# Opening of a two-layer backbone on one NeuronCore: the modulation in two halves of channels, two token pairs in between, and the transposed banks read by VectorE alone

## The chip, the core and the metric

The kernel runs on one core of one Trainium2 chip. A core has five engines that each work through their own instruction queue in order: TensorE (PE in the profile, with its weight loads as PEld), VectorE (DVE), ScalarE (ACT), GpSimd (POOL) and SyncE (SP, which here only starts transfers between the chip's memory and the on-chip memory). Semaphores hold an instruction back until what it needs is done. TensorE writes its results into eight banks of a small memory (PB in the profile) of 128 partitions by 512 fp32 words each; VectorE and ScalarE read them from there. The metric is the device time of one execution in microseconds, the median over runs.

## What is computed

Two layers over 1024 latent tokens and 256 context tokens of width 1024; layer 0 is windowed attention with sink logits, layer 1 latent attention. What the change touches is the very beginning of layer 0: a modulated normalization of all 1280 tokens, and its product with the value columns of the layer's input weight.

```python
def rms_norm(u, g):
    uf = u.astype(F32)
    y = uf * lax.rsqrt(jnp.mean(uf * uf, axis=-1, keepdims=True) + EPS)
    return (y * g.astype(F32)).astype(u.dtype)

def adaln(cond, w, bias):
    m = jax.nn.silu(cond) @ w + bias
    return jnp.split(m, 3, axis=-1)            # shift, scale, gate
...
    shift_x, scale_x, gate_x = adaln(c, ada_w[i], ada_b[i])
    shift_c, scale_c, gate_c = adaln(c_ctx, ada_w[i], ada_b[i])
    hx = rms_norm(x, norm_g[i]) * (1.0 + scale_x[:, None]) + shift_x[:, None]
    hc = rms_norm(ctx, norm_g[i]) * (1.0 + scale_c) + shift_c
    ...                                        # then h @ a_w_in[0], of which columns 1280:1536 are the values
```

All of it is fp32. A product is made from three matmuls of a high and a low part of each operand (high times high, low times high, high times low), so each tensor that TensorE multiplies is first split into its high part (a cast by ScalarE) and its low part (a subtraction).

## The kernel before

The whole kernel is laid out so that TensorE is never without work once the modulated tokens are there: the projections of layer 0, its attention, then layer 1. The stretch before that is the opening. Its order is written out by hand, for every engine, by the order of the calls in the code (a manual schedule): an engine takes its instructions in the order in which the lines issue them.

The opening handles the 1280 tokens as five pairs of 128-token tiles, `p` = 0 (context) to 4. The channels of a pair are worked in four groups `b` of 256 channels, so there are 20 groups, `g` = 0 to 19. The steps, by the names in the code:

- `ada_load(k)`, `ada_mm(k)`: 128 rows of the modulation weight (1 MB, two transfers of 512 KB) are loaded into one of three buffers, and TensorE multiplies them with both conditioning vectors; eight `k` make the sum over the 1024 input channels. `ada_cols` (L677 to L691) copies the sum, turns it to columns on TensorE and forms the factors A and B of all 1024 channels.
- `x_load(i)`, `norm(i)`: a tile of 128 tokens (512 KB) is loaded; ScalarE squares and sums it (L700), GpSimd makes the reciprocal root in two small instructions (L701, L702), and VectorE forms a diagonal matrix with it (L704), called the diagonal below.
- `turn(g)`: four matmuls of token tile times diagonal (L716) write 256 normalized channels of both tiles, transposed, into one bank. The first of them needs the pair's first diagonal, the next the second.
- `h_part(g)`: both halves of the bank are read twice, by ScalarE, which writes the high part of A·x+B directly (L728), and by VectorE, which writes A·x+B in fp32 (L729); the subtraction (L730) then gives the low part, on VectorE for even `g` and on GpSimd for odd `g`. Two engines that read the same bank are kept apart by semaphores, so the four readings of a group take turns.
- `v_part(g)`: twelve matmuls (L126 to L128, 256 wide) add the group's part of the values; after the fourth group of a pair, ScalarE and VectorE split the pair's values out of their bank into V, in four instructions. This split is called the V drain below.
- `w0_load`, `w0_cut`: the value columns of the weight (two transfers of 512 KB) and their split.

The loop at the end of the opening issues, at step `g`: `turn(g + 2)`, `h_part(g)`, then at the first two steps of each pair the `norm` of the next pair's tiles, and `v_part(g - 2)`. It runs after `ada_cols`, so that all 20 groups wait for the last row of the modulation weight. Some steps of the loop also start the transfers and the splits of the next weight block (`fetch(1)`, `next_item`). After the loop come the projections, which need the modulated tokens of pair 0 first.

Of the kernel before, what the change touches and what calls it, by code (L numbers as in the profile page):

```python
# [18 lines left out]
D = 1024  # L19
# [40 lines left out]
def kernel(ctx: ExitStack, tc: tile.TileContext, t, out, dbg=None):  # L60
# [593 lines left out]
    awr = Ring(F, [0, 8, 16], 2048)  # L654
    xs = Ring(F, [24, 28, 32, 36], 1024)
    w0 = f_at(40, 8, 256)
    am = f_at(22, 512)
    dg = Ring(F, [48, 48.5, 49, 49.5], 128)
    junk = f_at(50, 512).bitcast(BF16)
    hr = Ring(F, [16, 18, 20, 14], 512)  # L660
    PA, PM = PB[:, 6, :], PB[:, 7, :]
    turned = [0, 1, 2, 3, 6, 7]
    aw, xn, os = {}, {}, {}

    def ada_load(k):
        aw[k] = awr.next()
        for c in (0, 1024):
            load(out=aw[k][:, c : c + 1024], in_=t["ada_w"][0, k * 128 : k * 128 + 128, c : c + 1024])

    def ada_mm(k):  # L670
        for q in (0, 1, 2, 3):
            nc.tensor.matmul(
                PA[32 * q : 32 * q + 2], sc[:, k, :], aw[k][:, q * 512 : q * 512 + 512], start=k == 0, stop=k == 7
            )

    def ada_cols():
        nc.scalar.copy(am, PA)  # L677
        for j in range(4):
            nc.tensor.transpose(PM[:, j * 128 : j * 128 + 128], am[:, j * 128 : j * 128 + 128], ident)
        m = PM.rearrange("p (j q r) -> p q j r", j=4, q=4)[:, :, :, 0:2]  # L680

        def both(ap):
            return ap.rearrange("p (h j) c -> p h j c", h=2)

        def wide(ap):
            return ap.rearrange("p (h j) -> p h j", h=2).unsqueeze(3).to_broadcast([128, 2, 4, 2])

        A, B = both(ada0.A), both(ada0.B)
        nc.vector.tensor_add(A, m[:, 2:4], wide(adab[:, 0, 8:16]))
        nc.vector.scalar_tensor_tensor(A, A, 1.0, wide(ng[:, 0, :]), ALU.add, ALU.mult)  # L690
        nc.vector.tensor_add(B, m[:, 0:2], wide(adab[:, 0, 0:8]))  # L691

    def x_load(i):
        xn[i] = [xs.next(), None]
        load(out=xn[i][0], in_=src0(i))

    def norm(i):

        st = sm_ring()
        nc.scalar.activation(junk, xn[i][0], AF.Square, accum_out=st[:, 0:1])  # L700
        nc.gpsimd.tensor_scalar(st[:, 1:2], st[:, 0:1], 1.0 / D, EPS, ALU.mult, ALU.add)  # L701
        nc.gpsimd.tensor_tensor(st[:, 2:3], st[:, 1:2], mhalf, ALU.pow)  # L702
        xn[i][1] = dg.next()
        nc.vector.tensor_scalar_mul(xn[i][1], ident, st[:, 2:3])  # L704

    def bank(g):
        return shp(PB[:, turned[g % 6], :], 2, 256)

    def turn(g):

        p, b = g // 4, g % 4
# [8 lines left out]
    def h_part(g, eng):  # L720
        p, b = g // 4, g % 4
        w = 1 if p == 0 else 0
        h = shp(hr.next(), 2, 256)
        hi = hT[p][:, 0, 2 * b : 2 * b + 2, :]
        for kk in range(2):
            k = 2 * b + kk
            sa, sb = ada0.A[:, k, w : w + 1], ada0.B[:, k, w : w + 1]
            nc.scalar.activation(hi[:, kk], bank(g)[:, kk], AF.Identity, bias=sb, scale=sa)  # L728
            nc.vector.tensor_scalar(h[:, kk], bank(g)[:, kk], sa, sb, ALU.mult, ALU.add)  # L729
        eng.tensor_sub(hT[p][:, 1, 2 * b : 2 * b + 2, :], h, hi.bitcast(F32))  # L730

    def v_part(g):


        p, b = g // 4, g % 4
# [24 lines left out]
    nc.vector.memset(PA, 0.0)  # L760
    ada_load(0)
    load_small()
    ada_load(1)
    x_load(0)
    x_load(1)
    ada_load(2)
    w0_load(0)
    ada_mm(0)
    ada_mm(1)
    norm(0)  # L770
    norm(1)
    ada_mm(2)
    ada_load(3)
    w0_load(1)
    w0_cut(0)
    w0_cut(1)
    for g in range(2):
        turn(g)
    ada_load(4)
    ada_mm(3)  # L780
    ada_load(5)
    for g in range(2, 4):
        turn(g)
# [822 lines left out]
```

## Time and profile before

| | |
|---|---|
| median of three runs | 1646.34 us (1645.45 to 1647.07) |
| profiled execution, its own time | 1645.1 us |
| its span in the profile | 1643.1 us |
| TensorE busy in the span | 1583.2 us (96%) |
| factors A and B of all channels ready, first modulated bank | 34.77 us |
| last wait of TensorE in the opening ends | 98.35 us |
| granted clock of TensorE, mean of the span | 0.989 |

The page of the profile gives busy times by engine, a time line in 40 slices, the chain of work that ended last, and groups of instructions by line. A row of the time line reads: start, duration, engine, line, operation, what it writes and reads, how many instructions are merged, and in square brackets how long the engine was idle before and what ended that. A row of the table by windows has, after the window and its length, the busy microseconds and instruction counts of PE, PEld, DVE, ACT and POOL, then the granted clock of TensorE (1.00 is full speed), the share of the transfer engines' time and the transfer rate in GB/s.

### The profile page before, as it was taken

The page shows a single profiled execution, that of the slowest core. Times are in us where ns is not written, and L with a number is a line of the kernel's source. Part 1 is how long each engine was busy: PE and PEld are TensorE (multiplying, and loading weights), DVE is VectorE, ACT ScalarE, POOL GpSimd, SP SyncE. Part 2 cuts the span into 40 slices and gives each one's busy share as a digit, 9 for nine tenths or more (in the row PEclk, how much of TensorE's full clock was granted, in tenths as well). Part 3 has the DMA queues.
Part 4 walks back from the last instruction along what each step waited for, and adds up shares of the span by engine and source line. Part 5 has one row for each costly group of instructions (what it writes and reads, how often), then busy time and mean ns, then how long its engine had stood idle before and what let it go on. Part 6 is the DMA issues. An engine that isn't in the chain of part 4 may idle for free.

```text
span 1643.1 us, 23681 instructions
## 1 busy us (share of the span) xinstructions
PE 1583.2 (96%) x8232; PEld 1222.1 (74%) x8232; DVE 948.1 (58%) x1724; ACT 810.8 (49%) x1732; POOL 807.9 (49%) x865
## 2 busy tenths in 40 slices
PE   5899999989999999999999999999999999999998
PEld 1888888777888888878887887566756756666687
DVE  1567868837767777769444015655555455455354
ACT  2531212228777777777333334555555555555421
POOL 1442535415554334445245422786676777668510
PEclk8899999989999999999999999999999999999999
DMA  8325544573333322235127712210111111122151
GB/s 310 116 92 191 182 145 167 158 229 116 100 113 100 94 91 91 90 119 167 52 80 248 236 62 90 74 55 33 39 39 36 46 38 37 46 80 69 47 160 65
DMA packets 120351, 176.74 MB, mean 108 GB/s; under 512 B 11420, under 2 KB 71452, under 8 KB 120232
## 3 DMA queue, kind: packets, MB, share of 16 engines
q1 hardware_dynamic: 112952, 164.31, 30.6%
q10 hardware_dynamic: 7280, 10.92, 2.0%
q8 instruction: 65, 1.06, 0.3%
q14 instruction: 54, 0.44, 0.1%
HBM read 129.04 MB, written 46.15 MB: 107 GB/s over the span
## 4 chain that ended last, share of the span: by engine, by line
PE 81%; DVE 6%; ACT 4%; DMA 3%; issue 3%; POOL 2%; SPq 0%; ACTq 0%; POOLq 0%; DVEq 0%
PE PB L126 17%; PE PB L128 17%; PE PB L127 16%; PE PB L1279 9%; PE PB L570 5%; PE PB L1245 4%; PE PB L560 4%; PE PB L533 2%; PE PB L534 2%; DMA arena_f<-ada_w 2%; DVE arena_f L729 1%; DVE arena_f L344 1%; PE PB L1304 1%; DVE arena_r L122 1%; ACT arena_f L1264 1%
## 5 line engine op out<-in xcount | busy, mean ns | idle before, releaser
L126 PE MATMUL PB<-arena_r 128*128 128x512 f32 (+3 forms) x1632 | 608.0, 373 | 3.4 <-ACT arena_r L205 2.1
L127 PE MATMUL PB<-arena_r 128*128 128x512 f32 (+3 forms) x1632 | 595.9, 365 | 2.3 <-POOL arena_r L730 1.6
L128 PE MATMUL PB<-arena_r 128*128 128x512 f32 (+3 forms) x1632 | 594.3, 366 | 0.2 <-DVE arena_r L122 0.2
L126 PEld LDWEIGHTS PB<-arena_r 128*128 128x128 f32 (+1 forms) x1632 | 310.4, 190 | 90.7 <-issue 32.0
L1271 POOL TENSOR_TENSOR arena_f<-arena_f 128x512 f32<-128x512 f32 x252 | 327.5, 1300 | 75.1 <-ACT arena_f L1264 60.0
L128 PEld LDWEIGHTS PB<-arena_r 128*128 128x128 f32 (+1 forms) x1632 | 309.4, 190 | 48.9 <-DVE arena_r L122 0.4
L127 PEld LDWEIGHTS PB<-arena_r 128*128 128x128 f32 (+1 forms) x1632 | 310.4, 190 | 43.6 <-POOL arena_r L730 2.0
L1264 ACT ACTIVATE arena_f<-PB 128x512 f32<-128x512 f32 x320 | 189.1, 598 | 124.9 <-PE PB L128 113.2
L1249 DVE TENSOR_REDUCE arena_f<-PB 128x1 f32<-128x1280 f32 x128 | 190.4, 1488 | 103.9 <-PE PB L1245 101.4
L122 DVE TENSOR_TENSOR arena_r<-PB,arena_r 128x512 fp32r<-128x512 f32 (+4 forms) x255 | 163.0, 646 | 131.5 <-ACT arena_r L121 129.7
L122 POOL TENSOR_TENSOR arena_r<-arena_f,arena_r 128x512 fp32r<-128x512 f32 x80 | 111.2, 1403 | 176.3 <-ACT arena_r L121 160.7
L121 ACT CAST arena_r<-PB 128x512 fp32r<-128x512 f32 (+4 forms) x255 | 139.2, 550 | 78.8 <-PE PB L560 38.9
L540 DVE CUSTOM_DVE_ANT_0 arena_f<-PB,arena_f,small 128x256 f32<-128x256 f32 (+1 forms) x288 | 145.3, 523 | 32.1 <-PE PB L534 25.0
L1279 PE MATMUL PB<-arena_f 128*64 128x512 f32 x640 | 157.1, 600 | 0.0
L541 ACT ACTIVATE arena_f<-arena_f,small 128x640 f32<-128x640 f32 (+2 forms) x160 | 118.9, 744 | 28.2 <-DVE small L540 27.1
L570 PE MATMUL PB<-arena_r 128*128 128x512 f32 x336 | 120.9, 436 | 4.5 <-ACT arena_f L581 4.1
L344 DVE SCALAR_TENSOR_TENSOR arena_f<-arena_f,small 128x512 f32<-128x512 f32 x98 | 114.8, 1217 | 4.1 <-DMA arena_f<-ada_w 3.8
L560 PE MATMUL PB<-ident,arena_f 128*128 128x128 f32 x672 | 104.8, 273 | 0.4 <-ACT arena_f L541 0.3
L121 ACT CAST arena_r<-arena_f 128x512 fp32r<-128x512 f32 (+1 forms) x120 | 69.5, 607 | 71.4 <-DMA arena_f<-a_w_in 22.6
L1279 PEld LDWEIGHTS PB<-arena_f 128*64 128x64 f32 x640 | 43.5, 136 | 81.0 <-issue 79.5
L1245 PE MATMUL PB<-arena_r 96*128 96x512 f32 (+1 forms) x384 | 99.8, 367 | 0.3 <-DVE arena_f L1249 0.2
L560 PEld LDWEIGHTS PB<-ident,arena_f 128*128 128x128 f32 x672 | 82.6, 140 | 15.0 <-ACT arena_f L541 1.5
(163 smaller groups left out, 1734.1 us busy)
## 6 DMA issues: line engine op xcount, KB each, us to landing
arena_r<-q_d SPq DMA_DIRECT2D x148, 128.0 KB, 2.7
arena_f<-ada_w SPq DMA_DIRECT2D x64, 256.0 KB, 3.1
arena_f<-a_w_in SPq DMA_DIRECT2D x36, 256.0 KB, 2.9
arena_f<-ada_w SPq DMA_DIRECT2D x16, 512.0 KB, 8.7
arena_f<-x SPq DMA_DIRECT2D x16, 512.0 KB, 6.6
q_d<-arena_f SPq DMA_DIRECT2D x16, 512.0 KB, 3.0
qn_d<-arena_f SPq DMA_DIRECT2D x16, 512.0 KB, 5.1
arena_r<-qn_d SPq DMA_DIRECT2D x32, 256.0 KB, 3.5
```

The costliest lines, as they stand in the source:

```text
L121: nc.scalar.copy(hi, src)
L122: (lo_eng or nc.vector).tensor_sub(lo, src, hi.bitcast(F32))
L126: nc.tensor.matmul(o, ah, bh, start=first, stop=False)
L127: nc.tensor.matmul(o, al, bh, start=False, stop=False)
L128: nc.tensor.matmul(o, ah, bl, start=False, stop=last)
L560: nc.tensor.transpose(pt[:, h, :], self.Ps[h][:, ci * 128 : ci * 128 + 128], ident)
L570: nc.tensor.matmul(self.pv, V[:, self.chunks[ci], self.g, :], PT[:, s], start=ci == 0 and s == 0, stop=ci == self.m - 1 and s == 1,)
L1245: nc.tensor.matmul(psm[:, n0 : n0 + n], self.qT[0:96, 0, b * 128 : b * 128 + 128], kt[0:96, 0, n0 : n0 + n], start=True, stop=True,)
L1249: nc.vector.reduce_max(self.mx[:, 96 + b : 97 + b], psm[:, 0:TOK], AX.X, negate=True)
L1264: nc.scalar.activation(E, S, AF.Exp)
L1271: eng.tensor_add(self.acc, self.acc, E)
L1279: nc.tensor.matmul(self.pv[p : p + 64], Vq[:, c, self.h % 4, :], self.E.pop(c), start=c < 2, stop=c >= NT - 2)
```

## The change

**Modulation in two halves.** The modulation weight is loaded and multiplied as two halves `h` of 512 channels: `ada_load(h, k)` brings 512 KB in one transfer, with rows of 2 KB from two places in place of rows of 4 KB, into one of four buffers of that size, and `ada_mm(h, k)` has two matmuls where there were four; there are 16 of each. `ada_cols(h)` forms the factors of 512 channels, with a copy and transposes of 34 rows, by the method `set_cols` that layer 1 already uses, and runs twice.

**Two pairs in between.** The 20 groups get another order, held in `parts`: first the groups of channels 0 to 511 of pairs 0 and 1 (numbers 0 to 3), which need the first half only, then those of channels 512 to 1023 of the same pairs (4 to 7), then pairs 2 to 4 as before. Numbers 0 to 3, and `turn` of 4 to 7, are issued between the multiplications of the second half, and the loads of the second half are issued among them.

**Banks read by VectorE alone.** `h_part` has VectorE write A·x+B for both halves of the bank to on-chip memory, and ScalarE casts the 512 words from there to the high part in one instruction (L723). `h_low` does the subtraction one step later (L728), on GpSimd for three groups of four and on VectorE for the fourth. In the V drain, ScalarE makes both copies before VectorE makes both subtractions. `bank` uses four banks in place of six.

**Order of the loop.** `h_part(g)` stands ahead of `turn(g + 2)`; the diagonal is split off as `diag` and stands two steps after the pair's first `norm`, behind `h_part`. Buffers move to other places, and `x_load`, `fetch(1)` and the tables for the rotation are issued one or two steps later.

```diff
+    awr = Ring(F, [0, 4, 8, 12], 1024)
...
+    parts = [(p, b) for h in range(2) for p in range(2) for b in (2 * h, 2 * h + 1)]
+    parts += [(p, b) for p in range(2, NP) for b in range(4)]
...
+    def ada_load(h, k):
+        aw[h, k] = shp(awr.next(), 2, 512)
+        src = t["ada_w"][0, k * 128 : k * 128 + 128, 0 : 2 * D].rearrange("p (a c) -> p a c", a=2)
+        load(out=aw[h, k], in_=src[:, :, h * 512 : h * 512 + 512])
+    def ada_mm(h, k):
+        for a in range(2):
+            nc.tensor.matmul(PA[32 * a : 32 * a + 2], sc[:, k, :], aw[h, k][:, a, :], start=k == 0, stop=k == 7)
+    def ada_cols(h):
+        nc.scalar.copy(am[0:34], PA[0:34])
         for j in range(4):
+            nc.tensor.transpose(PM[:, 34 * j : 34 * j + 34], am[0:34, j * 128 : j * 128 + 128], ident[0:34, 0:34])
+        m = shp(PM, 4, 34)
+        ada0.set_cols(m[:, :, 32:34], 1, h)
+        ada0.set_cols(m[:, :, 0:2], 0, h)
...
+    def h_part(g):
+        p, b = parts[g]
         w = 1 if p == 0 else 0
+        hs[g] = shp(hr.next(), 2, 256)
         for kk in range(2):
             k = 2 * b + kk
             sa, sb = ada0.A[:, k, w : w + 1], ada0.B[:, k, w : w + 1]
-            nc.scalar.activation(hi[:, kk], bank(g)[:, kk], AF.Identity, bias=sb, scale=sa)
-            nc.vector.tensor_scalar(h[:, kk], bank(g)[:, kk], sa, sb, ALU.mult, ALU.add)
-        eng.tensor_sub(hT[p][:, 1, 2 * b : 2 * b + 2, :], h, hi.bitcast(F32))
+            nc.vector.tensor_scalar(hs[g][:, kk], bank(g)[:, kk], sa, sb, ALU.mult, ALU.add)
+        nc.scalar.copy(hT[p][:, 0, 2 * b : 2 * b + 2, :], hs[g])
+    def h_low(g, eng):
+        p, b = parts[g]
+        ks = slice(2 * b, 2 * b + 2)
+        eng.tensor_sub(hT[p][:, 1, ks, :], hs[g], hT[p][:, 0, ks, :].bitcast(F32))
...
         if b == 3:
+            o = PB[:, 4 + p % 2, :].rearrange("p (j h d) -> p j h d", j=2, h=4)
+            vs = V[:, 2 * p : 2 * p + 2]
             for j in range(2):
-                o = shp(PB[:, 4 + p % 2, j * 256 : j * 256 + 256], 4, 64)
-                split(V[:, 2 * p + j, :, 0:64], V[:, 2 * p + j, :, 64:128], o)
+                nc.scalar.copy(vs[:, j, :, 0:64], o[:, j])
+            for j in range(2):
+                nc.vector.tensor_sub(vs[:, j, :, 64:128], o[:, j], vs[:, j, :, 0:64].bitcast(F32))
...
+    ada_cols(0)
+    norm(2)
+    h_part(0)
+    norm(3)
+    h_part(1)
+    diag(2)
+    diag(3)
+    h_low(0, nc.gpsimd)
+    turn(2)
+    turn(3)
+    ada_mm(1, 0)
+    ada_load(1, 4)
+    for g in (2, 3):
+        h_part(g)
+        h_low(g - 1, nc.gpsimd)
+        turn(g + 2)
+        v_part(g - 2)
+        ada_mm(1, g - 1)
+        ada_load(1, g + 3)
+    h_low(3, nc.vector)
+    turn(6)
+    turn(7)
+    v_part(2)
+    ada_mm(1, 3)
+    ada_load(1, 7)
+    for i in range(4, 8):
+        x_load(i)
...
+    v_part(3)
+    for k in range(4, 8):
+        ada_mm(1, k)
+    ada_cols(1)
+    for g in range(4, NG + 2):
+        if g < NG:
+            h_part(g)
+        p = (g + 4) // 4
+        if g % 4 < 2 and p < NP:
+            norm(2 * p + g % 4)
+        if g % 4 == 2 and p < NP:
+            diag(2 * p)
+            diag(2 * p + 1)
+        if 5 <= g <= NG:
+            h_low(g - 1, nc.vector if g % 4 == 0 else nc.gpsimd)
+        if 6 <= g < NG - 2:
+            turn(g + 2)
...
+        if g >= 6:
+            v_part(g - 2)
```

On TensorE, from the fourth step of the modulation on, the order before is this (L672 is `ada_mm`, L716 `turn`, L679 the transposes of `ada_cols`, L126 the first matmul of `v_part`):

```order
L672 MATMUL PB<-arena_f,small 2x512 x4
L716 MATMUL PB<-arena_f 128x128 x8
L672 MATMUL PB<-arena_f,small 2x512 x16
L679 MATMUL PB<-ident,arena_f 128x128 x4
L716 MATMUL PB<-arena_f 128x128 x4
L126 MATMUL PB<-arena_r 128x256
```

And after, from the last two steps of the first half on (L675 is `ada_mm`, L680 the transposes, L711 `turn`):

```order
L675 MATMUL PB<-arena_f,small 2x512 x4
L680 MATMUL PB<-ident,arena_f 128x34 x4
L711 MATMUL PB<-arena_f 128x128 x8
L675 MATMUL PB<-arena_f,small 2x512 x2
L711 MATMUL PB<-arena_f 128x128 x4
L126 MATMUL PB<-arena_r 128x256
```

Two turns (those of tiles 2 and 3) now stand between the first half's columns and the first multiplication of the second half, and a turn and a `v_part` between each of the next ones; before, the last four steps of the modulation followed each other.

On VectorE, at the change from one pair to the next in the loop, the order before is this, here around the V drain of pair 0 (L729 reads a bank, L730 is the subtraction, L704 the diagonal, L122 the drain's subtraction):

```order
L730 TENSOR_TENSOR arena_r<-arena_f,arena_r 128x512
L704 TENSOR_SCALAR arena_f<-ident,small 128x128
L729 TENSOR_SCALAR arena_f<-PB,small 128x256 x2
L704 TENSOR_SCALAR arena_f<-ident,small 128x128
L122 TENSOR_TENSOR arena_r<-PB,arena_r 128x4x64 x2
L729 TENSOR_SCALAR arena_f<-PB,small 128x256 x2
```

And after, around the V drain of pair 1 (L722 reads a bank, L728 is the subtraction, L746 the drain's, L699 the diagonals of pair 3):

```order
L728 TENSOR_TENSOR arena_r<-arena_f,arena_r 128x512
L722 TENSOR_SCALAR arena_f<-PB,small 128x256 x2
L746 TENSOR_TENSOR arena_r<-PB,arena_r 128x4x64 x2
L722 TENSOR_SCALAR arena_f<-PB,small 128x256 x2
L699 TENSOR_SCALAR arena_f<-ident,small 128x128 x2
L722 TENSOR_SCALAR arena_f<-PB,small 128x256 x4
```

The second diagonal of the next pair stood ahead of the V drain; now both stand behind it, and behind the readings of one more bank.

On GpSimd, the loop's rows before are these, from a norm of pair 1 to the second of pair 2 (L701 and L702 are a norm, L730 a subtraction):

```order
L702 TENSOR_TENSOR small<-small 128x1
L730 TENSOR_TENSOR arena_r<-arena_f,arena_r 128x512
L701 TENSOR_SCALAR small<-small 128x1
L702 TENSOR_TENSOR small<-small 128x1
L730 TENSOR_TENSOR arena_r<-arena_f,arena_r 128x512
```

And after, the norms of pair 2 with what follows them (L692 and L693 are a norm, L728 a subtraction):

```order
L692 TENSOR_SCALAR small<-small 128x1
L693 TENSOR_TENSOR small<-small 128x1
L692 TENSOR_SCALAR small<-small 128x1
L693 TENSOR_TENSOR small<-small 128x1
L728 TENSOR_TENSOR arena_r<-arena_f,arena_r 128x512 x3
```

A subtraction stood between the two norms of a pair; now both norms stand first, and three subtractions directly behind the second.

More of the change, by code (lines that the diff above doesn't have):

```diff
@@ L650, in steps @@
             next(g, None)
[L654 to L658, printed above, removed]
+    awr = Ring(F, [0, 4, 8, 12], 1024)
+    xs = Ring(F, [16, 20, 24, 28], 1024)
+    w0 = f_at(32, 8, 256)
+    am = f_at(40, 512)
+    dg = Ring(F, [42, 42.5, 43, 43.5], 128)
     junk = f_at(50, 512).bitcast(BF16)
[L660 removed]
+    hr = Ring(F, [44, 46, 48, 32], 512)
@@ L661 @@
     PA, PM = PB[:, 6, :], PB[:, 7, :]
[L662 to L677, printed above, removed]
-        for j in range(4):
[L679 to L691, printed above, removed]
@@ L775 @@
+    ada_load(0, 6)
+    for i in range(2):
+        norm(i)
+    for i in range(2):
+        diag(i)
+    ada_mm(0, 3)
+    ada_load(0, 7)
     w0_cut(0)
     w0_cut(1)
[L777 to L783, printed above, removed]
+    ada_mm(0, 4)
+    ada_mm(0, 5)
+    x_load(2)
+    x_load(3)
+    turn(0)
+    turn(1)
+    ada_mm(0, 6)
+    ada_mm(0, 7)
+    ada_load(1, 0)
+    w0_load(1)
+    for k in (1, 2, 3):
+        ada_load(1, k)
```

70 lines of the change are left out of this document (25 added, 45 removed).

## The prediction

> **What bounds the kernel now.** I read the table by windows first, to see where TensorE is the bound and where it isn't.
>
> ```profile
> span 1643.1 us, 23681 instructions
> ```
>
> ```profile
> core 0: us, PE busy (x) PEld busy (x) DVE busy (x) ACT busy (x) POOL busy (x), PEclk, DMA share, GB/s
> ...
> 40.00:45.00 5.00, 1.92 (x9) 1.92 (x10) 2.04 (x5) 2.38 (x5) 2.01 (x3) 0.50 0.00 0
> ...
> 65.00:70.00 5.00, 2.43 (x11) 2.44 (x12) 1.66 (x5) 2.17 (x7) 2.00 (x3) 0.69 0.27 109
> 70.00:75.00 5.00, 5.00 (x30) 5.00 (x29) 3.74 (x5) 3.49 (x8) 4.52 (x4) 0.63 0.43 133
> ...
> 100.00:110.00 10.00, 10.00 (x68) 9.24 (x67) 6.71 (x9) 2.85 (x6) 3.09 (x3) 1.00 0.33 109
> 110.00:120.00 10.00, 10.00 (x46) 8.28 (x45) 7.50 (x11) 1.24 (x2) 8.06 (x6) 1.00 0.58 198
> ```
>
> From 100 us on TensorE is busy without a gap; before that it is often idle, and its clock is at half speed in places. So a microsecond by which the opening ends earlier or later is a microsecond of the kernel, and everything hangs on when TensorE ends the last `v_part`. Next the time line of TensorE: its waits in the opening, and its pace between them.
>
> ```profile
> 43.09 1.65 PE L716 MATMUL PB<-arena_f 128*128 128x128 f32 x6 [3.42 <-DVE arena_f L704]
> ...
> 54.67 0.94 PE L716 MATMUL PB<-arena_f 128*128 128x128 f32 x6 [0.51 <-DVE arena_f L704]
> ...
> 59.21 1.06 PE L716 MATMUL PB<-arena_f 128*128 128x128 f32 x8
> 60.02 0.36 PE L126 MATMUL PB<-arena_r 128*128 128x256 f32 x1
> ...
> 61.54 1.06 PE L716 MATMUL PB<-arena_f 128*128 128x128 f32 x8
> ...
> 67.57 1.65 PE L716 MATMUL PB<-arena_f 128*128 128x128 f32 x6 [3.32 <-DVE arena_f L704]
> ...
> 81.75 0.94 PE L716 MATMUL PB<-arena_f 128*128 128x128 f32 x6 [1.80 <-DVE arena_f L704]
> ...
> 92.96 0.39 PE L127 MATMUL PB<-arena_r 128*128 128x256 f32 x1 [0.31 <-POOL arena_r L730]
> ...
> 95.37 0.39 PE L127 MATMUL PB<-arena_r 128*128 128x256 f32 x1 [0.72 <-DVE arena_r L730]
> ...
> 98.35 0.39 PE L127 MATMUL PB<-arena_r 128*128 128x256 f32 x1 [1.28 <-POOL arena_r L730]
> ```
>
> A turn takes 60.02 − 59.21 = 0.81, a `v_part` 61.54 − 60.02 = 1.52. From 43.1 there are 16 turns and 20 `v_part`, 13.0 + 30.4 = 43.4, which ends at 86.5. The later waits add 0.51 + 3.32 + 1.80 + 0.31 + 0.72 + 1.28 = 7.9, which makes 94.4. The last `v_part` (its second matmul starts at 98.35, eleven at 0.12 follow) ends at 99.7. The missing 5.3 are what the slow clock cost, after the two waits of over 3 us: 2.65 a spell. As ends for one spell I take what the windows from 65 to 75 lost, (0.31 + 0.37) × 5 = 3.4 us of clock, part of it under the wait, and half of that, 1.7. The wait of 1.80 left the clock at full speed. This account of before is what I repeat for the changed order.
>
> **The part that gets cheaper.** VectorE and ScalarE wait for each other over the banks:
>
> ```profile
> ACT arena_r L728 <- DVE arena_f L729: 20.7, 20, 2.2
> DVE arena_f L729 <- ACT arena_r L728: 13.9, 22, 0.6
> ```
>
> That goes: ScalarE no longer reads the banks of the groups. The rows for the new order's pieces, by groups of the opening, and one row for two readings in a row:
>
> ```profile
> L729 DVE TENSOR_SCALAR arena_f<-PB,small 128x256 f32<-128x256 f32 x40 | 21.3, 542 | 14.0 <-ACT arena_r L728 13.9
> L730 POOL TENSOR_TENSOR arena_r<-arena_f,arena_r 128x512 fp32r<-128x512 f32 x10 | 12.8, 1280 | 28.4 <-DVE arena_f L729 28.4
> ...
> L121 ACT CAST arena_r<-arena_f 128x512 fp32r<-128x512 f32 x8 | 4.5, 616 | 5.8 <-DMA arena_f<-a_w_in 5.8
> L121 ACT CAST arena_r<-PB 128x256 fp32r<-128x256 f32 x10 | 3.7, 371 | 11.2 <-DVE arena_r L122 5.8 <-PE PB L128 5.4
> L122 DVE TENSOR_TENSOR arena_r<-PB,arena_r 128x256 fp32r<-128x256 f32 x9 | 3.8, 422 | 5.2 <-ACT arena_r L121 5.2
> ```
>
> ```profile
> 46.48 1.00 DVE L729 TENSOR_SCALAR arena_f<-PB,small 128x256 f32<-128x256 f32 x2 [0.64 <-ACT arena_r L728]
> ```
>
> A group then has 1.0 on VectorE, 0.6 on ScalarE and 1.3 on GpSimd, all under TensorE's 2.33. So between pairs nothing but TensorE's own pace should count; at the changes of pair and in the two column steps the chains through several engines count, and those I add up.
>
> **The first half.** From the time line:
>
> ```profile
> 20.44 1.04 PE L672 MATMUL PB<-arena_f,small 128*2 128x512 f32 x8
> ...
> 31.86 1.03 PE L672 MATMUL PB<-arena_f,small 128*2 128x512 f32 x4 [0.25 <-DMA arena_f<-ada_w]
> 32.93 0.59 ACT L677 COPY arena_f<-PB 128x512 f32<-128x512 f32 x1 [10.19 <-PE PB L672]
> ...
> 34.77 0.56 ACT L728 ACTIVATE arena_r<-PB,small 128x256 fp32r<-128x256 f32 x1 [1.25 <-DVE small L691]
> ...
> 36.41 1.04 ACT L700 ACTIVATE arena_f<-arena_f 128x1024 bf16<-128x1024 f32 x1
> ...
> 37.63 0.23 POOL L701 TENSOR_SCALAR small<-small 128x1 f32<-128x1 f32 x1 [14.07 <-ACT arena_f L700]
> 37.95 0.55 POOL L702 TENSOR_TENSOR small<-small 128x1 f32<-128x1 f32 x1
> 38.53 0.28 DVE L704 TENSOR_SCALAR arena_f<-ident,small 128x128 f32<-128x128 f32 x1 [0.72 <-POOL small L702]
> ```
>
> The last piece that the first half needs is the eleventh 512 KB transfer of SP's queue (eight of the modulation, two of tokens, one of the value weight); before, the eleventh is the second part of step 3, which was there at 20.44. I take the rate as unchanged for rows of 2 KB; a tenth less would make this and all that follows some 1.8 later. One step of 1.0 (row 31.86), then the copy, transposes and factors, 34.77 − 32.89 = 1.9: the first bank can be read at 23.3, 11.5 us earlier than before.
>
> TensorE's next work is the turn of tile 3's pair, which needs diagonal 3, and that is late: two readings 1.0, cast 0.6, square and sum 1.2 (36.41 to 37.63), GpSimd 0.9 (37.63 to 38.53), diagonal 0.3, so 27.3. Behind GpSimd's norm its queue now holds the first subtraction, ready to go. What that does to a diagonal is shown later in the trace, by VectorE's one-input operation with GpSimd idle and with it busy:
>
> ```profile
> 101.57 0.87 DVE L342 TENSOR_SCALAR arena_f<-arena_f,small 128x512 f32<-128x512 f32 x2
> ...
> 137.08 2.80 DVE L342 TENSOR_SCALAR arena_f<-arena_f,small 128x512 f32<-128x512 f32 x2
> ...
> 135.61 3.98 POOL L122 TENSOR_TENSOR arena_r<-arena_f,arena_r 128x512 fp32r<-128x512 f32 x3 [3.33 <-ACT arena_r L121]
> ```
>
> Two operations took 2.80 in place of 0.87, and they ended with GpSimd's three. So a diagonal may wait up to one subtraction, 1.3; where both become ready at the same moment either may win, and I take half: TensorE goes on at 28.0 (27.3 to 28.6).
>
> [...]
>
> **The second half.** From there TensorE has 6 turns (4.9), 4 `v_part` (6.1) and 8 steps of `ada_mm` at 1.0, together 19.0. It has then been idle over 4 us, so a slow spell comes with it (2.65): 49.6. The four last loads leave only when `ada_mm(1, 0)` to `(1, 3)` have freed their buffers, in TensorE's order; the last goes out 1.5 + 4.0 = 5.5 before the end and must have landed 1.0 before it.
>
> ```profile
> arena_f<-ada_w SPq DMA_DIRECT2D x64, 256.0 KB, 3.1
> ...
> arena_f<-x SPq DMA_DIRECT2D x16, 512.0 KB, 6.6
> ```
>
> At 3.1 for half its size it is hidden; at the 6.6 of token tiles, which queued behind each other, it would cost 2.1, an end of the range. So the loads' pace, which set 31.86 before, no longer sets the second half; the turns and `v_part` put between its steps do. SP's later transfers (tiles 4 to 7) wait behind the last load, and land before ScalarE comes to them.
>
> **The rest.** Columns 1.9: bank 4 can be read at 51.5, 16.7 us later than the first bank before, with 4 groups of 20 done. The turn of pair 2 needs diagonal 5: readings 1.0; on ScalarE cast, square, cast, square, 0.6 + 1.1 + 0.6 + 1.2; GpSimd 0.9; diagonal 0.3, with 0 to 1.3 for the subtraction that starts behind the norm: 57.2 to 58.5, I take 57.9. Then 12 turns and 16 `v_part`, 9.7 + 24.3 = 34.0: 91.9. Waits of TensorE: at pair 3 the V drain stands ahead of the diagonals on VectorE, and it waits for TensorE's last `v_part`, so TensorE waits for two copies (0.7), two subtractions (0.8), two readings (1.0) and two diagonals (0.5), 3.0, and up to 1.3 more for GpSimd: 4.0. At pair 4 the same, with GpSimd less far behind, 3.0. At the end drain, readings, cast and subtraction, 0.7 + 0.8 + 1.0 + 0.6 + 1.3 = 4.4, less two `v_part` that run meanwhile: 1.4. Sum 8.4: 100.3. Slow spells at 2.65 follow the waits at pairs 2 and 3 for sure, at pair 4 by even odds: 6.6. The opening ends at 106.9 in place of 99.7.
>
> The removed taking of turns is worth little by itself, since TensorE's 2.33 a group was near VectorE's pace. The next weight block's splits and the rotation's tables shift with the loop and stay under it.
>
> **Sum**: 1645.1 + 7.2 = 1652.3, say 1652. The profiled execution was the fast end of before (median 1646.34), and the slow spells, which vary with where the waits fall, are a likely reason; against that median it is +5.7, or 0.34%.
>
> **Rivals.**
> Short spells: the clock comes back sooner. At 1.7 a spell (the low end) and with only the three sure ones they cost 5.1 in place of 9.3: 1648, no change. For it: the spells of before differ among themselves, since the share of a wait that counts is unknown. Against: the waits here, 4 to 7 us, are longer than those that gave 2.65.
> [...]
>
> VectorE ahead: at 1.0 a group VectorE has the diagonals of pairs 3 and 4 ready before TensorE asks. Then 4.0 + 3.0 go, with 4.0 of slow spells, and 1652.3 becomes 1641.3, faster. It decides if the diagonals overtake the V drain. For it: VectorE's shorter group. Against: the order, in which drain and bank reading stand ahead of them; and the 3.32 and 1.80 of before, where less stood ahead.
>
> Worse: every diagonal waits a full subtraction (1.5 more), all spells cost 3.4 (2.6 more) and the last load costs 2.1: 1658.
>
> **Chances and range.** 0.2%, or 3.3 us, is about what a measurement here can tell from no change. Forecast (1649.7 to 1656) 0.55, short spells 0.18, VectorE ahead 0.14, worse 0.13. So slower 0.68, same 0.18, faster 0.14. The range leaves out the faster case and reaches over the others: 1645.5 to 1657.
>
> **What would show it.** Right: the first bank read at about 23, a TensorE wait of 4 to 6 for a diagonal behind it, last step of the modulation near 49, a wait of 6 to 8 at pair 2, waits of 3 to 4 at pairs 3 and 4 behind the drain, the first 512-wide matmuls some 7 us later than before. Wrong: if the second half ends near 40, if the diagonals come ahead of TensorE, or if the clock stays at 1.00 in the windows after those waits.

## The result

The changed kernel takes 1653.48 us, the median of five runs (1651.83 to 1654.45), against 1647.07 (1645.45 to 1647.46) for the kernel before beside it: ratio 1.0040, 95% interval 1.0026 to 1.0055. It is slower by 0.4%. The profiled execution (1653.19 us, span 1651.1) stands 8.0 above the one of before (span 1643.1).

The time lies in the opening and is handed through one to one. The first read of a 512-wide bank, which belongs to the projections and comes 6.0 behind the last `v_part`, starts at 114.54 in place of 105.72, 8.8 later; from there to the end of the span it is 1536.6 and 1537.4. Over all fourteen kernels below that rest is 1536.6 to 1539.0, while the opening's length varies by 32 us.

The clock, in the table by windows of the changed kernel (columns as before):

```profile
25.00:30.00 5.00, 1.32 (x4) 1.03 (x5) 2.87 (x6) 2.18 (x4) 3.09 (x5) 0.62 0.76 280
30.00:35.00 5.00, 5.00 (x28) 3.80 (x27) 2.44 (x5) 1.72 (x4) 1.83 (x2) 0.70 0.03 5
...
50.00:55.00 5.00, 0.78 (x6) 0.32 (x4) 3.21 (x9) 2.50 (x5) 0.17 (x1) 0.85 1.03 399
55.00:60.00 5.00, 2.21 (x9) 1.92 (x9) 2.47 (x4) 2.35 (x5) 4.10 (x7) 0.50 0.12 39
60.00:65.00 5.00, 5.00 (x31) 5.00 (x30) 0.00 (x0) 0.08 (x1) 0.90 (x1) 0.62 0.01 3
...
70.00:75.00 5.00, 0.51 (x4) 0.31 (x3) 3.16 (x6) 2.42 (x6) 4.10 (x6) 0.90 0.50 196
75.00:80.00 5.00, 4.58 (x20) 4.28 (x21) 4.03 (x6) 3.12 (x6) 2.76 (x3) 0.50 0.01 3
...
90.00:95.00 5.00, 4.85 (x29) 4.85 (x29) 2.80 (x7) 1.79 (x3) 2.55 (x2) 0.66 0.11 42
```

From 25 us on there are four slow spells (stretches at a granted clock near half) behind waits at the four pairs 1 to 4, where before had two (0.50 from 40 to 45, 0.69 and 0.63 from 65 to 75). The time line of the changed kernel, TensorE first:

```profile
20.99 1.89 PE L675 MATMUL PB<-arena_f,small 128*2 128x512 f32 x8
23.55 0.44 PE L680 MATMUL PB<-ident,arena_f 34*128 34x34 f32 x4 [0.68 <-ACT arena_f L678]
26.65 0.80 PE L711 MATMUL PB<-arena_f 128*128 128x128 f32 x2 [2.66 <-DVE arena_f L699]
29.48 3.36 PE L711 MATMUL PB<-arena_f 128*128 128x128 f32 x14 [2.03 <-DVE arena_f L699]
...
46.74 3.60 PE L675 MATMUL PB<-arena_f,small 128*2 128x512 f32 x16
...
56.03 0.79 PE L711 MATMUL PB<-arena_f 128*128 128x128 f32 x2 [4.57 <-DVE arena_f L699]
58.58 1.65 PE L711 MATMUL PB<-arena_f 128*128 128x128 f32 x6 [1.75 <-DVE arena_f L699]
...
74.78 0.80 PE L711 MATMUL PB<-arena_f 128*128 128x128 f32 x2 [4.49 <-DVE arena_f L699]
76.00 1.65 PE L711 MATMUL PB<-arena_f 128*128 128x128 f32 x6 [0.42 <-DVE arena_f L699]
90.15 1.27 PE L711 MATMUL PB<-arena_f 128*128 128x128 f32 x8 [2.63 <-DVE arena_f L699]
```

But for the short one at 23.55, all of these waits are for diagonals (L699). VectorE's and GpSimd's rows show why the diagonals are late:

```profile
24.50 1.90 DVE L722 TENSOR_SCALAR arena_f<-PB,small 128x256 f32<-128x256 f32 x4
26.32 0.28 DVE L699 TENSOR_SCALAR arena_f<-ident,small 128x128 f32<-128x128 f32 x1
28.15 1.28 DVE L699 TENSOR_SCALAR arena_f<-ident,small 128x128 f32<-128x128 f32 x1 [1.55 <-POOL small L693]
...
55.69 0.29 DVE L699 TENSOR_SCALAR arena_f<-ident,small 128x128 f32<-128x128 f32 x1 [0.84 <-POOL small L693]
57.25 1.28 DVE L699 TENSOR_SCALAR arena_f<-ident,small 128x128 f32<-128x128 f32 x1 [1.27 <-POOL small L693]
...
71.84 0.76 DVE L746 TENSOR_TENSOR arena_r<-PB,arena_r 128x256 fp32r<-128x256 f32 x2 [2.32 <-ACT arena_r L744]
73.42 2.53 DVE L699 TENSOR_SCALAR arena_f<-ident,small 128x128 f32<-128x128 f32 x2
...
89.82 0.47 DVE L699 TENSOR_SCALAR arena_f<-ident,small 128x128 f32<-128x128 f32 x2
```

```profile
28.08 2.48 POOL L728 TENSOR_TENSOR arena_r<-arena_f,arena_r 128x512 fp32r<-128x512 f32 x2
...
57.18 3.72 POOL L728 TENSOR_TENSOR arena_r<-arena_f,arena_r 128x512 fp32r<-128x512 f32 x3
...
72.16 3.71 POOL L728 TENSOR_TENSOR arena_r<-arena_f,arena_r 128x512 fp32r<-128x512 f32 x3
```

A diagonal alone takes 0.28. Where GpSimd's subtraction has just begun (28.08, 57.18, 72.16), it takes 1.28, and two take 2.53; at 89.82, with GpSimd idle, two take 0.47. At pair 3 the V drain (71.84) stands ahead of them, and it waited 2.32 for ScalarE's copies of TensorE's last `v_part`. The first diagonals of pairs 1 and 2 are late for neither reason: at 26.32 the diagonal stands behind four readings, and at 55.69 it waits for the norm. Before them TensorE waits 2.66 and 4.57.

### The profile page after: what moved, and what is told of

It reads as the page before. It is cut to its first block, busy times and chain, and to the rows that moved or that the text cites. A ratio compares the mean times of both kernels' runs of the same rounds, so it can differ in the third digit from the quotient of the medians.

```text
span 1651.1 us, 23676 instructions
## 1 busy us (share of the span) xinstructions
PE 1587.6 (96%) x8236; PEld 1224.5 (74%) x8236; DVE 944.9 (57%) x1722; ACT 802.0 (49%) x1713; POOL 813.3 (49%) x870
## 4 chain that ended last, share of the span: by engine, by line
PE 82%; DVE 5%; ACT 4%; issue 4%; POOL 3%; DMA 2%; ACTq 0%; POOLq 0%; SPq 0%; DVEq 0%
PE PB L126 17%; PE PB L128 17%; PE PB L127 17%; PE PB L1317 9%; PE PB L570 5%; PE PB L1283 4%; PE PB L560 4%; PE PB L533 2%; PE PB L534 2%; PE PB L711 1%; DMA arena_f<-ada_w 1%; DVE arena_f L344 1%; PE PB L675 1%; PE PB L1342 1%; ACT arena_f L1302 1%
## 5 line engine op out<-in xcount | busy, mean ns | idle before, releaser
L126 PE MATMUL PB<-arena_r 128*128 128x512 f32 (+3 forms) x1632 | 607.9, 373 | 4.4 <-ACT arena_r L205 2.1
L126 PEld LDWEIGHTS PB<-arena_r 128*128 128x128 f32 (+1 forms) x1632 | 309.9, 190 | 93.1 <-issue 32.9
L122 DVE TENSOR_TENSOR arena_r<-PB,arena_r 128x512 fp32r<-128x512 f32 (+4 forms) x245 | 158.7, 655 | 125.9 <-ACT arena_r L121 124.1
L122 POOL TENSOR_TENSOR arena_r<-arena_f,arena_r 128x512 fp32r<-128x512 f32 x80 | 111.1, 1403 | 174.7 <-ACT arena_r L121 155.6
L121 ACT CAST arena_r<-PB 128x512 fp32r<-128x512 f32 (+4 forms) x245 | 135.5, 557 | 67.7 <-PE PB L560 39.1
L1283 PE MATMUL PB<-arena_r 96*128 96x512 f32 (+1 forms) x384 | 99.7, 367 | 0.3 <-DVE arena_f L1287 0.2
```

The lines of the kernel that those rows point to most:

```text
L121: nc.scalar.copy(hi, src)
L122: (lo_eng or nc.vector).tensor_sub(lo, src, hi.bitcast(F32))
L126: nc.tensor.matmul(o, ah, bh, start=first, stop=False)
L1283: nc.tensor.matmul(psm[:, n0 : n0 + n], self.qT[0:96, 0, b * 128 : b * 128 + 128], kt[0:96, 0, n0 : n0 + n], start=True, stop=True,)
```

## The experiments

The theory after the result: the change loses its head start at the diagonals (by the drain ahead of them and by GpSimd's subtraction beside them), in the slow clock behind those waits, and in the second half of the modulation, which goes at TensorE's order; the single reader is worth little. Each kernel was timed in turn with the kernel before, whose median was 1647.0 to 1647.7 throughout. "Opening" is the start of the first read of a 512-wide bank in the profiled execution, whose time can lie off the median: it was 1651.46 with idle matmuls, the highest of eleven, and 1646.94 with the subtractions on VectorE, the lowest of eleven.

| kernel | median us | ratio to before (95%) | opening us |
|---|---|---|---|
| before | 1647.07 | | 105.72 |
| changed | 1653.48 | 1.0040 (1.0026 to 1.0055) | 114.54 |
| halves, two readers | 1661.70 | 1.0091 (1.0078 to 1.0104) | 121.32 |
| one piece, one reader | 1646.74 | 0.9995 (0.9986 to 1.0004) | 105.68 |
| changed, subtractions on VectorE | 1648.78 | 1.0013 (1.0005 to 1.0022) | 108.54 |
| changed, diagonals ahead | 1644.92 | 0.9989 (0.9981 to 0.9998) | 105.84 |
| changed, idle matmuls | 1648.85 | 1.0009 (1.0000 to 1.0018) | 112.08 |
| one piece, one reader, subtractions on VectorE | 1642.66 | 0.9973 (0.9963 to 0.9984) | 103.24 |
| the same, diagonals ahead | 1630.36 | 0.9900 (0.9886 to 0.9914) | 91.79 |
| changed, steps in the wait | 1649.90 | 1.0020 (1.0011 to 1.0029) | 110.47 |
| changed, both mends | 1645.02 | 0.9982 (0.9973 to 0.9991) | 105.20 |
| one piece, diagonals ahead, idle matmuls | 1629.42 | 0.9888 (0.9872 to 0.9903) | 90.72 |
| the same, weight later | 1629.06 | 0.9887 (0.9874 to 0.9901) | 89.42 |
| one piece, diagonals ahead, two readers | 1644.85 | 0.9984 (0.9975 to 0.9993) | 104.83 |

**Halves without the single reader**

```diff
         for kk in range(2):
...
+            nc.scalar.activation(hT[p][:, 0, k, :], bank(g)[:, kk], AF.Identity, bias=sb, scale=sa)
             nc.vector.tensor_scalar(hs[g][:, kk], bank(g)[:, kk], sa, sb, ALU.mult, ALU.add)
-        nc.scalar.copy(hT[p][:, 0, 2 * b : 2 * b + 2, :], hs[g])
```

> The changed kernel with one part undone: the banks are read twice again, by ScalarE (high part) and VectorE (fp32), in turns; halves, order of the loop, drain and subtraction one step later stay. Theory, by the step "worth little by itself": VectorE's pace of a group stays under TensorE's 2.33 us, so the opening ends within 1.5 us of the changed kernel's, 1652 to 1655. Rival: with two readers a group holds both engines for about 2.1 us (two readings of 0.5 on each, one after another), and at every change of pair two squarings of 1.2 stand in ScalarE's queue in between, so the chains at pairs 2, 3 and 4 and the end get some 2 us longer each: 1658 to 1663, and the single reader was a gain that the halves needed.

1661.70, as the rival said. Without the single reader the halves are 8.2 slower still. TensorE's time line of this kernel, pairs 2 to 4:

```profile
63.34 0.79 PE L711 MATMUL PB<-arena_f 128*128 128x128 f32 x2 [9.61 <-DVE arena_f L699]
...
80.17 0.80 PE L711 MATMUL PB<-arena_f 128*128 128x128 f32 x2 [4.47 <-DVE arena_f L699]
...
95.30 0.80 PE L711 MATMUL PB<-arena_f 128*128 128x128 f32 x2 [3.35 <-DVE arena_f L699]
```

With both diagonals of a pair counted, pair 2's wait is 10.0 in place of 6.3: there three groups are read in a row with both squarings in between, and the readings in turns lengthen that chain most. At pair 1 it is 6.2 in place of 4.7, at pair 4 3.8 in place of 2.6, and at pair 3 it is the same, 4.9.

**The single reader alone.** In the kernel before, `h_part`, `h_low` and the V drain of the changed kernel, and in the loop:

```diff
-            h_part(g, nc.gpsimd if g % 2 else nc.vector)
+            h_part(g)
+        if 1 <= g <= NG:
+            h_low(g - 1, nc.vector if g % 4 == 0 else nc.gpsimd)
```

> The kernel before with the other part alone: the modulation stays in one piece and the loop keeps its order, but VectorE alone reads the banks, ScalarE casts from on-chip memory, the subtraction stands one step later (GpSimd for three of four) and the V drain has both copies first. Theory: worth little, since the waits of before at the diagonals (3.42, 3.32 and 1.80) come from the norm chain, which stays: 1643 to 1648. Rival: the taking of turns was what made the diagonals late, and those waits and the two slow spells go (some 8 us): 1637 to 1641.

1646.74, no difference, as the theory said, but for another reason. Of its eight diagonals in the loop seven took 1.28 to 1.30, where in the kernel before all eight took 0.28 or 0.29. VectorE's and GpSimd's rows of this kernel:

```profile
38.77 1.28 DVE L704 TENSOR_SCALAR arena_f<-ident,small 128x128 f32<-128x128 f32 x1 [2.64 <-POOL small L702]
43.60 1.28 DVE L704 TENSOR_SCALAR arena_f<-ident,small 128x128 f32<-128x128 f32 x1 [2.65 <-POOL small L702]
```

```profile
38.18 0.55 POOL L702 TENSOR_TENSOR small<-small 128x1 f32<-128x1 f32 x1
38.70 1.26 POOL L733 TENSOR_TENSOR arena_r<-arena_f,arena_r 128x512 fp32r<-128x512 f32 x1
```

The subtraction, one step later than before, is ready when the norm is done, and starts in the same moment as the diagonal. Before, it waited for VectorE's reading and came 2 us behind the norm. So the norm chain did not "stay": the reader's gain was eaten by a new wait, as the run without GpSimd's subtractions below bears out.

**Subtractions on VectorE, in the changed kernel.** Every `h_low` on `nc.vector`.

> The changed kernel with all subtractions of the groups on VectorE, so that GpSimd has only the norms and the splits of the weights there. Theory (a diagonal beside a subtraction on GpSimd is shut out): the diagonals that took 1.28, 1.28 and 2.53 (two) take 0.28 each, which takes 1.0, 1.0 and 2.0 off TensorE's waits: 1648 to 1650.5. Rival 1: VectorE, with 0.65 more in three of four groups, comes late with the readings and gives it back: 1652 to 1656. Rival 2: the long diagonals were long for another reason (their own second wait on GpSimd): they stay at 1.28, and the time within 1.5 of the changed kernel's 1653.5.

1648.78, 4.7 less, as the theory said. All diagonals are short (pair 3's, VectorE's row of this kernel):

```profile
69.96 0.47 DVE L699 TENSOR_SCALAR arena_f<-ident,small 128x128 f32<-128x128 f32 x2
```

**Diagonals ahead of the drain**

```diff
-        if g % 4 < 2 and p < NP:
-            norm(2 * p + g % 4)
-        if g % 4 == 2 and p < NP:
+        if g % 4 == 0 and p < NP:
+            norm(2 * p)
+            norm(2 * p + 1)
+        if g % 4 == 1 and p < NP:
             diag(2 * p)
             diag(2 * p + 1)
```

> The changed kernel with both norms of a pair at the pair's first step of the loop and both diagonals at its second, so that they stand ahead of the V drain on VectorE. Theory (the diagonals were late because of what stood ahead of them, the drain that waits for TensorE): the wait of 5.3 at pair 3 falls to about 2, the one of 2.6 at pair 4 to under 1.5, and the slow spells behind them (about 2.5 each) go or halve: 1642 to 1647. Rival: the norm itself is late (ScalarE's squarings behind the casts, then GpSimd), VectorE waits for it with the readings queued behind, and the waits of TensorE stay in another form: 1651 to 1654.

1644.92: 8.6 less than the changed kernel, and a little under the kernel before. TensorE's waits from pair 3 on, all of them:

```profile
69.99 0.49 PE L711 MATMUL PB<-arena_f 128*128 128x128 f32 x2 [0.72 <-DVE arena_f L699]
72.17 1.65 PE L711 MATMUL PB<-arena_f 128*128 128x128 f32 x6 [1.68 <-DVE arena_f L699]
95.64 0.39 PE L126 MATMUL PB<-arena_r 128*128 128x256 f32 x1 [0.21 <-ACT arena_r L723]
96.98 0.39 PE L127 MATMUL PB<-arena_r 128*128 128x256 f32 x1 [0.96 <-POOL arena_r L728]
```

Pair 3 waits 2.4 in place of 4.9, pair 4 not at all, and the spell behind pair 4 is gone (1.00 in each window from 80 to 95). The place of the norms and diagonals in the queues is worth more than the whole of what the change lost (6.4).

**Idle matmuls in the waits.** They write an unused bank, and nothing reads it.

```diff
+    def idle_mm(n, b):
+        for _ in range(n):
+            nc.tensor.matmul(PB[:, b, :], wt[0][:, 0, 2, 0:128], wt[0][:, 0, 0:2, :], start=True, stop=True)
...
+    idle_mm(10, 5)
     turn(2)
...
+        if g in (6, 10, 14):
+            idle_mm({6: 18, 10: 16, 14: 9}[g], 6)
```

> The changed kernel with idle matmuls (512 wide, result not used) in four of TensorE's waits: 10 ahead of the turn of tiles 2 and 3, 18 ahead of pair 2's first turn, 16 ahead of pair 3's, 9 ahead of pair 4's, each set short enough to end before the awaited diagonal. Nothing else is moved, so only the granted clock behind the waits can change. Theory (a slow spell costs 2 to 2.65 us, four of them): 1643 to 1647, with the windows behind the waits at 0.9 and more. Rival, short spells or spells that only fill later waits: 1649 to 1652. Rival, no effect: TensorE's pace is not what the next diagonal waits for, 1653 as the changed kernel.

1648.85, 4.6 less: between the ranges, at the edge of that of the rival with short spells. In the profiled execution only two of the four spells went. Its windows:

```profile
30.00:35.00 5.00, 5.00 (x20) 3.07 (x20) 2.86 (x6) 2.27 (x4) 1.93 (x2) 0.52 0.02 5
...
60.00:65.00 5.00, 5.00 (x26) 5.00 (x25) 0.13 (x1) 0.62 (x1) 1.60 (x2) 0.50 0.00 0
...
75.00:80.00 5.00, 3.38 (x27) 3.08 (x27) 4.68 (x7) 2.22 (x5) 2.76 (x3) 1.00 0.02 5
...
90.00:95.00 5.00, 5.00 (x46) 5.00 (x45) 2.84 (x6) 1.86 (x3) 2.73 (x3) 1.00 0.34 110
```

The two that stayed lie behind the wait for a second diagonal (2.35 and 2.07), which the idle matmuls, all ahead of the first, don't fill. From pair 3's second diagonal to pair 4's turn it takes 11.98 (77.22 to 89.20) in place of 14.15 (76.00 to 90.15), so the spell of pair 3 costs 2.2. From pair 4's turn to the end of the opening it takes 22.88 in place of 24.39, so the spell of pair 4 costs 1.5. Ahead of pair 3's second diagonal 1.2 was lost, which leaves 2.5 of the opening in this execution. How the 4.6 of the median is made up is not shown, since the other executions have no trace.

**One piece, single reader, subtractions on VectorE.** The kernel with the single reader alone, and `h_low(g - 1, nc.vector)`.

> The kernel before with the single reader, and all subtractions of the groups on VectorE. Theory: the single reader alone gained nothing because GpSimd's subtraction then stood right behind the norm and made seven of eight diagonals 1.28 instead of 0.28 us; without it pairs 1, 3 and 4 gain 2.0, 2.0 and 1.0 and pair 2 its 0.5: 1640 to 1643. Rival: VectorE's extra 0.65 a group makes readings and diagonals late, 1645 to 1648.

1642.66, 4.1 less than with GpSimd's subtractions: the long diagonals had hidden what the single reader is worth. All eight diagonals take 0.29.

**One piece, diagonals ahead.** On top of the last one, with `diag` split off from `norm` as in the changed kernel:

```diff
+    norm(2)
+    norm(3)
     NG = 4 * NP
...
-        if b < 2 and p + 1 < NP:
-            norm(2 * p + 2 + b)
+        if b == 0 and 0 < p and p + 1 < NP:
+            norm(2 * p + 2)
+            norm(2 * p + 3)
+        if b == 1 and p + 1 < NP:
+            diag(2 * p + 2)
+            diag(2 * p + 3)
```

> As the run with the single reader and all subtractions on VectorE, modulation in one piece; also the diagonals split off and put one step behind both norms of a pair (ahead of the V drain), and the norms of tiles 2 and 3 ahead of the first group's cast on ScalarE. Theory (halves are not needed once the diagonals are early): pair 1's second diagonal is there near 39 in place of 42.7, the waits at pairs 2 to 4 fall to under 1 each, one slow spell stays: the opening ends near 86 to 89 in place of 99.7, 1633 to 1638. Rival: the norm chain (ScalarE, GpSimd) is late whatever the order, 1639 to 1644.

1630.36: a larger gain than expected, 1.0% under the kernel before and 23 under the changed one. Its waits of TensorE for diagonals, in the view of waits and on the time line:

```profile
PE PB L720 <- DVE arena_f L708: 4.4, 3, 3.6
```

```profile
37.72 1.87 PE L720 MATMUL PB<-arena_f 128*128 128x128 f32 x8 [3.59 <-DVE arena_f L708]
...
68.09 0.49 PE L720 MATMUL PB<-arena_f 128*128 128x128 f32 x2 [0.32 <-DVE arena_f L708]
69.10 0.94 PE L720 MATMUL PB<-arena_f 128*128 128x128 f32 x6 [0.52 <-DVE arena_f L708]
```

4.4 in all, where the changed kernel had 18.6, and no slow spell after 45 (1.00 in every window of the opening from there on).

**Steps of the second half in the wait**

```diff
+    for k in range(3):
+        ada_mm(1, k)
+        ada_load(1, k + 4)
     turn(2)
     turn(3)
-    ada_mm(1, 0)
-    ada_load(1, 4)
```

(The same steps go from the loop behind.)

> The changed kernel with the first three multiplications of the second half ahead of the turn of tiles 2 and 3 instead of between the groups behind it. Theory (the second half is bound by TensorE's order, and TensorE's waits of 2.7 and 2.0 there stand empty): three steps of 1.0 go into them, the last step of the modulation ends near 47 in place of 50.3, and the slow spell behind shrinks: 1648.5 to 1651. Rival: the loads are not there yet (the second and third land after 26), the turn is held up and the time stays at 1653 or rises to 1655.

1649.90, 3.6 less. The transposes of the second half start at 48.21 in place of 51.02, though the loads held the steps up twice, by 1.13 and 1.46. Of these 2.8, 0.7 came from the first half (its transposes start at 22.85 in place of 23.55). The other 2.1 show that TensorE's order sets the length of the second half.

**Both mends in the changed kernel.** Diagonals ahead, and all `h_low` on VectorE.

> The changed kernel with both mends: diagonals ahead of the V drain, and all subtractions of the groups on VectorE. It has what the one-piece run at 1630.4 has, except that the modulation is in halves with two pairs in between. Theory (the halves themselves cost: their second half ends near 49 and pair 2's wait of 6 and its slow spell stay): 1640 to 1644, some 10 above the one-piece run. Rival (the halves cost nothing once the diagonals are early): 1629 to 1634.

1645.02, 14.7 above the one-piece run: on the theory's side, but above its range. The second mend added nothing to the first. In this execution GpSimd's split of the next weight block, and a memset behind it, stood beside pair 4's second diagonal (80.67, 1.74), TensorE waited 1.04 and 1.97 there, and the first half ended 0.9 later than in the run with the diagonals alone. How the mends share the rest is open. The 14.7 is not shown to be the price of the halves alone: besides them, this kernel has four banks for six and `h_part` ahead of `turn`, and ScalarE comes to the norms of tiles 3 to 5 only behind a group's cast, where the one-piece kernel has the norms of its first pair in the loop ahead of the first cast. TensorE waits 2.67 and 1.04 for the diagonals of pair 1 here and 4.50 and 0.39 for those of pair 2, against 3.59 and nothing there. Halves with these norms moved ahead were not run.

**Idle matmuls in the one-piece kernel.** 13 `idle_mm` at `g == 2`, ahead of `turn(4)`.

> The one-piece run at 1630.4 with 13 idle matmuls in the one wait over 2 us that it has left, ahead of pair 1's first turn. There the turn and the part of the values behind the wait took 4.0 (37.72 to 41.72) where they take 2.33 at full clock, so the theory (a spell costs what its slow work loses, and nothing else makes it up) expects 1.7 less: 1628 to 1629.3. Rival, VectorE's 1.5 a group or the later diagonals set the pace there anyway: 1630 to 1631.5.

1629.42, between the two ranges. The spell is gone in the profiled execution (the windows from 35 to 45 are at 1.00, where they were at 0.80 and 0.86): turn and `v_part` take 2.43 (38.22 to 40.65) in place of 4.00, which prices this spell at 1.6. But the diagonals came 0.5 later (37.89) in this execution, and the times of the two kernels can't be told apart (intervals 0.9872 to 0.9903 and 0.9886 to 0.9914).

**Value weight later.** On top of the last one: `w0_load(1)` behind `x_load(3)`, and `w0_cut(2)`, `w0_cut(3)` at `g == 1`.

> The run with idle matmuls in the one-piece kernel, and the second transfer of the value weight (512 KB) moved behind the tokens of tiles 2 and 3, with its split behind the second group. Theory (the transfers set the first bank, at 1.28 a 512 KB): the factors and with them everything behind come 1.3 earlier: 1626.5 to 1628.2. Rival: the weight's last quarter is now late (its low part after about 38.5) or its split on VectorE holds up the readings: 1628.5 to 1631.

1629.06: not in the theory's range but in the rival's, and it can't be told from the run before it (1629.42). The opening is 1.3 shorter in the profile, the theory's amount, but that compares with an execution at 1631.26, the highest of four. The rival's hold-up is there too: VectorE's split (37.00, 1.36) stands ahead of the readings of the third group (38.28), and TensorE waits 0.18 at 39.92. This is the lowest median of the study, 1.1% under the kernel before.

**Two readers in the one-piece kernel.** The diff of the first experiment, on the one-piece kernel with the diagonals ahead.

> The one-piece run at 1630.4 with one part undone: the banks are read twice in turns again, by ScalarE and VectorE; early diagonals and subtractions on VectorE stay. Theory (the single reader is worth little in the kernel before only because the diagonals were later still; with them early the readings are the pace): a group takes 2.1 in turns and 0.65 for the subtraction, 2.75 on VectorE's chain where TensorE needs 2.33, which over 20 groups and with longer chains at the changes of pair makes 1640 to 1650. Rival (the reader is worth nothing, early diagonals do it all): 1630 to 1634.

1644.85, as the theory said. With early diagonals and the subtractions on VectorE the single reader is worth 14.5; alone it was worth nothing.

## Why the prediction was right, and where not

The time came out 1.5 above the forecast, slower as forecast, by the mechanism forecast. Its steps:

| step | predicted | measured |
|---|---|---|
| first bank read | 23.3 | 24.50 |
| turn of tiles 2 and 3 goes on | 28.0 | 29.48 |
| last `ada_mm` ends | 49.6 | 50.34 |
| bank 4 read | 51.5 | 52.05 |
| turn of pair 2 goes on | 57.9 | 58.58 |
| waits at pair 3, pair 4, end | 4.0, 3.0, 1.4 | 4.9, 2.6, 1.2 |
| slow spells of pairs 2 to 4 | 6.6 | 7.2 |
| end of the opening | 106.9 | 108.5 |

The last measured number is 99.7 + 8.8; the 7.2 is what is left of 108.5 − 58.6 after 34.0 of work and 8.7 of waits. The time came nearer to the forecast than the opening did (1.6 late), partly by luck: in the profiled execution the rest was 0.8 shorter than before (1536.6 for 1537.4).

- **First bank**, 1.2 late, and not by the rate of the transfers that the prediction set as its term: TensorE takes the last two steps of the first half (20.99) without a wait for a transfer. Behind a wait of 3.08 TensorE's clock fell in the first half too (0.56 in the window from 15 to 20), which the sum did not have. Twelve matmuls took 5.29 there. They took 4.27, at a clock of 0.87, in the run with subtractions on VectorE, whose code is the same up to that place, and there the first bank is read at 22.93, before the predicted 23.3:

```profile
13.47 5.29 PE L675 MATMUL PB<-arena_f,small 128*2 128x512 f32 x12 [3.08 <-DMA arena_f<-ada_w]
```

```profile
13.23 4.27 PE L675 MATMUL PB<-arena_f,small 128*2 128x512 f32 x12 [2.96 <-DMA arena_f<-ada_w]
```

- **The wait of a diagonal for a subtraction** was put at half its price. It came at full price, 1.28 in place of 0.28, at the diagonals of tiles 3 and 5 and twice at pair 3 (2.53 for two); the diagonals of tiles 2 and 4 and those of pair 4, beside which no subtraction stood, were free of it. With the full price at every diagonal, 1.5 more by the prediction's last rival, the sum would have been 1653.8.
- **Second half and spells.** The second half was 0.8 shorter than predicted (20.9 for 21.65). The 2.65 a spell was a little high: the last three came to 2.4 each (7.2 in all), with 2.2 measured behind pair 3, 1.5 behind pair 4, and 1.6 for the one of the one-piece kernel. Pair 4's spell, taken at even odds, came. The rival of short spells (1.7 each, three of them) was near the price of some and too low for the sum. What the prediction set against it, that the waits here are longer than those that gave 2.65, is a misreading: the first spell of before stood behind waits of 4.65 and 3.42 (38.87 and 43.09).
- **VectorE ahead** did not happen, for the reason named, the order; the run with norms and diagonals ahead of the drain shows that the order decides most of it (1644.9, where the rival's price gave 1641; pair 3 still waits 2.4).
- **"Worth little by itself"**, of the single reader, is the step whose reason failed. The number holds for the reader alone (0.9995), but the paces of the engines were not why: the subtraction, which goes one step later with it, had moved beside the diagonals. In the halves the reader is worth 8.2, in the one-piece kernel with early diagonals 14.5. The prediction did not ask what the same reader would do without the halves, and so missed that a good part of the change was held down by where subtractions and diagonals stand.

## What to carry to other kernels

Before work is rearranged to start earlier, look at what each engine's queue has ahead of the small instruction that releases the next stage: here moving norms and 0.28 us diagonals ahead of a drain was worth 8.6 us, while the changed kernel, whose first bank is read 10 us earlier, was slower. Undo and redo the parts of a change one by one and in pairs, since a part that measures nothing alone may be the one that pays when a wait beside it is gone. A wait of 2 to 5 us could cost TensorE some 1.5 to 2.4 us more here, in slow clock behind it.

## What the runs showed of the hardware

- Same code, different clock. In seven executions whose code is the same up to there, the transposes of the first half started at 21.97 to 23.60; the three late ones (23.46, 23.55, 23.60) are those with a clock of 0.55 to 0.58 in the window from 15 to 20, the others had 0.69 to 0.87. The three late ones also had the longest waits ahead of it (3.08 to 3.31, the others 2.52 to 2.96). But it isn't the length of the wait alone that decides: 2.70 was followed by a clock of 1.00 (one piece, one reader, subtractions on VectorE, the first row below), 2.07 with 18 idle matmuls shortly ahead by 0.50 (changed, idle matmuls, the second row), and 1.04 and 1.97 one after the other by 1.00 (changed, both mends). What else decides, no row shows.

```profile
66.56 0.94 PE L716 MATMUL PB<-arena_f 128*128 128x128 f32 x6 [2.70 <-DVE arena_f L704]
```

```profile
59.28 1.65 PE L711 MATMUL PB<-arena_f 128*128 128x128 f32 x6 [2.07 <-DVE arena_f L699]
```

- The readings of a bank took no longer beside GpSimd's subtractions, where a diagonal took longer (1.28 in place of 0.28). In the changed kernel two readings wholly beside GpSimd's subtractions (58.45) took 0.98, and two with GpSimd idle 1.00 (31.16). Six readings, beside GpSimd's subtractions for over half of their time, took 2.79 (run with the diagonals ahead, VectorE, then GpSimd) and 2.80 with GpSimd idle (changed kernel, 52.05):

```profile
70.84 1.27 DVE L699 TENSOR_SCALAR arena_f<-ident,small 128x128 f32<-128x128 f32 x1 [0.90 <-POOL small L693]
72.03 0.74 DVE L746 TENSOR_TENSOR arena_r<-PB,arena_r 128x256 fp32r<-128x256 f32 x2
72.70 2.79 DVE L722 TENSOR_SCALAR arena_f<-PB,small 128x256 f32<-128x256 f32 x6
```

```profile
70.77 2.49 POOL L728 TENSOR_TENSOR arena_r<-arena_f,arena_r 128x512 fp32r<-128x512 f32 x2
74.41 1.29 POOL L728 TENSOR_TENSOR arena_r<-arena_f,arena_r 128x512 fp32r<-128x512 f32 x1 [1.15 <-ACT arena_r L723]
```

- VectorE's subtraction of two on-chip operands took 1.65 in place of 0.68 beside GpSimd's split (run with subtractions on VectorE, 73.36).
